# Other places for tiles, slices and loads in the projections and scan of a hybrid encoder block

## The chip, the cores and the metric

The kernel runs on one core of a Trainium2 chip, as one program in one launch. The metric is the device time of one execution in microseconds (us). Before the change three executions took 2998.09, 3004.99 and 3011.6 us; their median, 3004.99 us, is the time to predict against. The profile is one further execution with its own time.

## The reference, cut to what matters

One encoder block over 1040 tokens (16 meta tokens, then 1024), width 1024. The part that the change touches is the input projection and the two-way state-space scan that is fed by it:

```python
u = rms_norm(h, w_norm_mix)
proj = einsum('btd,dk->btk', u, w_in)              # 72.5 column tiles of 128
c = depthwise_conv(conf_a * sigmoid(conf_g), 31)   # "conf": 8 tiles
xbc = silu(depthwise_conv(xbc, 7))                 # 16 tiles of x, 4 of B, 4 of C
gates = sigmoid(proj[gate])                        # 16 tiles
# z: 16 tiles, gates the scan's output; dt: 64 columns
# scan, per group g (4), chunk c (9), both directions:
cb = einsum('lgn,sgn->gls', C, B)                  # C times B, masked for each direction
y_diag = (cb * decay) @ (x * dt)
states = B.T @ (decay_to_end * x * dt);  y_off = C @ prev_state * exp(a_cs)
y = rms_norm((y_f + y_b + D * x) * silu(z))
```

Behind it come the output products of both branches, the merge, and a mixture of 16 experts with 128 MB of weights for each of its three matrices.

## The kernel before, in words

A Tile program: instructions are written in Python order, and the framework's scheduler places them on the engines by their priority (`tc.high_priority(offset=...)` moves an instruction ahead). What then stands on an engine runs strictly in that order.

**Front.** The 1040 tokens are handled in nine chunks (`TOK`: 16, then eight of 128). Per chunk: load `xt` (four buffers, loads on SP's and ACT's queues in turn), a Square with a sum on ACT (L265), square root and reciprocal, a scaling on DVE (L267), eight transposes on PE (L272), and the split into an upper and a lower f16 half, `uh` by ACT (L274) and `ul` by DVE (L275). `Columns` feeds the weights: a group of three column tiles of `w_in` is loaded at once, `scale` finds a power of two per tile (Squares on ACT L198, a product L204, small steps on DVE), `convert` makes the two f16 halves (ACT L225, DVE L226).

**Projections.** A column tile is made in three "thirds", one for each of three stretches of about 346 tokens. A third is 24 matmuls into one of three PSUM banks (`mm`): eight k-steps times three products of halves (L97 to L99). `do_dt` takes dt's 64 columns first and builds the decays. `first` is the list of tiles made before the scan, `plan[0]` to `plan[2]` carry the tiles of groups 1 to 3 beside the scan of groups 0 to 2, `plan[3]` what is left beside the scan of group 3.

- `x_(g, i)`, a channel tile (i of 0 to 3 are x, 4 is B, 5 is C): evacuated by ACT to `pre`, then six taps of the 7-wide convolution on DVE (L385, tile `po`), a Silu on ACT (L386). Eight thirds later PE transposes `po` (`turn`, L400, into a bank of `mm`), ACT copies the result (`xt`, L404), and it is written to `xk_d`, from which the next group's scan loads it.
- `c_(j)`, a conf tile: six thirds, then 30 taps of the 31-wide convolution on DVE (L339, tile `co`). They are kept in a list, and every step of the scan takes 2, 4, 3 or 6 of them, by group.
- `z_` and `g_` are evacuated by ACT (z with one product on DVE, L362).

**Scan.** 18 steps for each group. A step has `within` (the masked `cb`, L602 and L606; the decays `row`, L611 to L614; products `py`, L626) and `state` (`yo` L665, `st` L671, the state `S` on DVE). Between the two `fill` lets PE make as many thirds as the step's share of the group's plan. `cb` had a PSUM tile of its own in a pool with one buffer; its two masks are made by DVE.

Of the kernel before, what the change touches and what calls it, by code (L numbers as in the profile page):

```python
# [7 lines left out]
F32 = mybir.dt.float32  # L8
# [4 lines left out]
AF = mybir.ActivationFunctionType  # L13
# [19 lines left out]
NTT = len(TOK)  # L33
# [12 lines left out]
def tile_block(ctx, tc, x, meta_tokens, w_norm_mix, w_in, w_conf_dw, b_conf_dw, conf_ln_g, conf_ln_b,  # L46
# [100 lines left out]
    def power(dst, src, up, down):  # L147

        dve.tensor_scalar(dst[:, down], src, 32.0, 2.0 ** -110, op0=OP.mult, op1=OP.max)
        di = dst.bitcast(I32)  # L150
        dve.tensor_scalar(di[:, down], di[:, down], 23, 23, op0=OP.logical_shift_right, op1=OP.logical_shift_left)
        dve.tensor_scalar(di[:, up], di[:, down], -1.0, float(268 << 23), op0=OP.mult, op1=OP.add)
        dve.tensor_scalar(di[:, down], di[:, down], float(14 << 23), None, op0=OP.subtract)
# [10 lines left out]
    with tpool("upool", side="right") as upool, tpool("stage", bufs=4, side="right") as stage, \  # L164
# [11 lines left out]
        class Columns:  # L176
# [52 lines left out]
            def take(self, col):  # L229

                n = self.at
                assert self.order[n] == col
                self.at += 1
                if n == 0:
                    self.load()
                    self.scale(0, turned)
                    self.convert(0)
                if n % self.G == 0:
                    self.load()
                if n % self.G == 1:  # L240
                    self.scale(n - 1 + self.G)
                self.convert(n + 1)
                wh, wl, sc = self.split.pop(n)
                return wh, wl, sc[:, 2:3], sc[:, 3:4]

        columns = Columns()
        wtile = columns.take


        with tpool("a_sb", bufs=2) as sb, tpool("a_ps", bufs=4, space=PSUM) as aps:  # L250
            wmix = sb.tile([P, D], F32, name="wmix", bufs=1)
            nc.scalar.dma_start(wmix, w_norm_mix[0].partition_broadcast(P))
            wabs = sb.tile([P, D], F32, name="scr")
            act.activation(out=wabs, in_=wmix, func=AF.Abs)
            wmax = sb.tile([P, 1], F32, name="wmax", bufs=1)
            dve.tensor_reduce(out=wmax, in_=wabs, axis=AX.X, op=OP.max)

            power(su, wmax, slice(0, 1), slice(1, 2))
            for c, (t0, L) in enumerate(TOK):
                xt = sb.tile([P, D], F32, name="xt", bufs=4)  # L260
                eng = nc.scalar if c % 2 else nc.sync
                eng.dma_start(xt[:L], meta_tokens if c == 0 else x[0, t0 - 16:t0 - 16 + L])
                scr = sb.tile([P, D], F32, name="scr")
                ss = sb.tile([P, 1], F32, name="ss")
                act.activation(out=scr[:L], in_=xt[:L], func=AF.Square, accum_out=ss[:L])  # L265
                rsqrt_mean(ss[:L], ss[:L], D)
                dve.scalar_tensor_tensor(xt[:L], xt[:L], ss[:L], wmix[:L], op0=OP.mult, op1=OP.mult)  # L267
                for q in range(2):
                    ps = aps.tile([P, 4, P], F32, name="tp")
                    for j in range(4):  # L270
                        k = 4 * q + j
                        turned = pe.transpose(ps[:, j, :L], xt[:L, k * P:(k + 1) * P], ident[:L, :L])  # L272
                    uu = uh[:, 4 * q:4 * q + 4, t0:t0 + L]
                    act.activation(out=uu, in_=ps[:, :, :L], func=AF.Copy, scale=su[:, 0:1])  # L274
                    dve.scalar_tensor_tensor(ul[:, 4 * q:4 * q + 4, t0:t0 + L], ps[:, :, :L], su[:, 0:1], uu,  # L275
                                             op0=OP.mult, op1=OP.subtract)
            prow = sb.tile([36, D], F32, name="prow", bufs=1)
            nc.gpsimd.dma_start(prow[:TK], w_conf_dw[0])
            nc.gpsimd.dma_start(prow[31:32], b_conf_dw)
            nc.gpsimd.dma_start(prow[32:33], conf_ln_g)  # L280
            nc.gpsimd.dma_start(prow[33:34], conf_ln_b)
            nc.gpsimd.dma_start(prow[34:36], w_ssm_norm[0].rearrange("(r c) -> r c", r=2))
            srow = sb.tile([8, 3 * D], F32, name="srow", bufs=1)
            nc.gpsimd.dma_start(srow[:TS], w_ssm_conv[0])
            nc.gpsimd.dma_start(srow[7:8], b_ssm_conv)
            db = sb.tile([P, H], F32, name="db", bufs=1)
            nc.gpsimd.dma_start(db, ssm_d[0].partition_broadcast(P))
            for hh in range(2):
                dve.tensor_copy(d2[64 * hh:64 * hh + 64], db[64 * hh:64 * hh + 64, hh::2])
            ps = aps.tile([P, KD, 36], F32, name="tp")  # L290
            for j in range(KD):
                pe.transpose(ps[:, j], prow[:, j * P:(j + 1) * P], ident[:36, :36])
            dve.tensor_copy(cp, ps)
            dve.tensor_scalar_mul(cp[:, :, 0:TK], cp[:, :, 0:TK], 0.5)
            ps = aps.tile([P, 24, 8], F32, name="tp")
            for j in range(24):
                pe.transpose(ps[:, j], srow[:, j * P:(j + 1) * P], ident[:8, :8])
            dve.tensor_copy(sp, ps)

        def proj(wsplit, t0, n):  # L300
            ps = mps.tile([P, 512], F32, name="mm")
            wh, wl = wsplit[:2]
            mm3(ps[:, :n], lambda k: wh[:, k, :], lambda k: wl[:, k, :],
                lambda k: uh[:, k, t0:t0 + n], lambda k: ul[:, k, t0:t0 + n], KD)
            return ps[:, :n]

        def soon():
            return tc.high_priority(offset=1000)
# [102 lines left out]


        def do_dt(b1, b1ps):
            w = wtile(OFF_DT)
            v, ve = [b1.tile([64, T], F32, name=n_, bufs=1) for n_ in ("dtv", "dte")]
            for t0, n in NCH0:
                act.activation(out=v[:, t0:t0 + n], in_=proj(w, t0, n)[:64], func=AF.Copy,
                               scale=w[2][:64])
            dtb = b1.tile([P, 2, 64], F32, name="dtb", bufs=1)
            for i, a in enumerate((ssm_dt_bias, ssm_a_log)):  # L420
                nc.gpsimd.dma_start(dtb[:, i], a[0].rearrange("d h -> (d h)").partition_broadcast(P))
# [61 lines left out]
                nc.gpsimd.dma_start(ecs_d[1:, hh].rearrange("c q l -> q c l"),  # L483
                                    ve[hh::2, NMETA:].rearrange("h (c l) -> h c l", l=P))


        def x_(g, *tiles):
            return [("xbc", g, i) for i in tiles]

        def z_(*js):  # L490
            return [("z", j) for j in js]

        def g_(*js):
            return [("gate", j) for j in js]

        def c_(j):
            return [("conf", j)]

        first = x_(0, 4) + c_(0) + x_(0, 5, 0) + g_(0) + x_(0, 1, 2) + g_(1) + x_(0, 3) + z_(0, 1, 2)
        plan = [x_(1, 4) + z_(3) + x_(1, 5, 0) + c_(1) + x_(1, 1) + g_(2) + x_(1, 2, 3) + g_(3, 4) + z_(4, 5),  # L500
                x_(2, 4) + z_(6) + c_(2) + z_(7) + x_(2, 5, 0, 1) + g_(5) + x_(2, 2, 3) + c_(3) + z_(8, 9),
                x_(3, 4) + z_(10) + x_(3, 5) + z_(11) + c_(4) + x_(3, 0, 1) + g_(6) + x_(3, 2, 3) + g_(7, 8) + z_(12, 13),
                z_(14, 15) + c_(5) + g_(9) + c_(6) + g_(10, 11) + c_(7) + g_(12, 13, 14, 15)]
        makers = {"conf": do_conf, "xbc": xbc_tile, "z": z_tile, "gate": gate_tile}
        columns.order.append(OFF_DT)
        for kind, *a in first + [i for p_ in plan for i in p_]:
            if kind == "conf":
                columns.order += [a[0] * P, D + a[0] * P]
            elif kind == "xbc":
                columns.order.append(OFF_XBC + (4 * a[0] + a[1], 16 + a[0], 20 + a[0])[max(0, a[1] - 3)] * P)  # L510
            else:
                columns.order.append((OFF_Z if kind == "z" else OFF_GATE) + a[0] * P)

        def thirds(items):
            for kind, *a in items:
                for _ in makers[kind](*a):
# [5 lines left out]
        with tpool("b1") as b1:  # L522
# [12 lines left out]
            with tpool("s2", bufs=2) as s2, tpool("sps", bufs=1, space=PSUM) as sps:  # L535
# [45 lines left out]
                    nc.gpsimd.dma_start(yz_d[g][:, :, t0:t0 + L].rearrange("i p t -> p i t"), xa)  # L581

                shared = {}

                def within(g, c, d):

# [820 lines left out]
```

## Time and profile before

| | us |
|---|---|
| median of three executions | 3004.99 |
| the profiled execution | 2988.87 |
| its span in the profile | 2987.1 |
| PE busy, of the span | 2750.6 (92%) |
| DVE busy | 2240.1 (75%) |
| ACT busy | 1713.3 (57%) |

PE is TensorE, DVE is VectorE, ACT is ScalarE, POOL is GpSimd, SP is SyncE. Matmuls are pipelined, so two rows may overlap; a wait stands in brackets at the end of a row of a timeline, with what ended it. The granted clock is TensorE's, as a share of its full speed.

### The profile page before, as it was taken

The numbers are of one execution on the slowest core, as the hardware profiler recorded it, in microseconds if no ns is written. First come the engines' busy times: TensorE is split into PE (matmuls) and PEld (weight loads), VectorE is DVE, ScalarE is ACT, GpSimd is POOL, SyncE is SP. The second block draws the span as 40 slices with busy tenths as digits, with TensorE's granted clock in tenths as the row PEclk, the third lists the DMA queues.
The fourth block names the chain that finished last, engine by engine and source line by source line (L and its number), as shares of the span: only waits on it lengthen the run. The fifth ranks groups of instructions, "written<-read, shape, count | busy, mean of one in ns | idle before, by whom it ended". The sixth has DMA issues, their size and how long they took to land. (4 is left out here: it accounts for less than half of the span.)

```text
span 2987.1 us, 65478 instructions
## 1 busy us (share of the span) xinstructions
PE 2750.6 (92%) x27584; PEld 2359.5 (79%) x27584; DVE 2240.1 (75%) x3023; ACT 1713.3 (57%) x2549; POOL 616.6 (21%) x688
## 2 busy tenths in 40 slices
PE   6989989989997998989998889999999999999995
PEld 4656656655665666989967889999999999999995
DVE  6867896998896799988456677777767676777663
ACT  6567656565665542444223656766666666666743
POOL 2131132132123113330000002222211112222213
PEclk8999989999998999999999899999999999999997
DMA  5356576565566554424345889999999999999994
GB/s 146 96 160 198 173 214 202 156 197 181 181 180 207 161 176 131 161 61 139 107 141 181 301 291 332 337 327 333 336 322 330 325 332 322 332 338 330 334 323 141
DMA packets 337783, 689.77 MB, mean 231 GB/s; under 512 B 38241, under 2 KB 98049, under 8 KB 337481
## 3 DMA queue, kind: packets, MB, share of 16 engines
q1 hardware_dynamic: 284784, 528.74, 51.4%
q0 software_dynamic: 42624, 125.45, 14.7%
q10 hardware_dynamic: 10080, 31.40, 3.3%
q8 instruction: 216, 3.54, 0.5%
q14 instruction: 79, 0.65, 0.1%
HBM read 610.48 MB, written 75.01 MB: 229 GB/s over the span
## 5 line engine op out<-in xcount | busy, mean ns | idle before, releaser
L97 PE MATMUL gu<-xT,wh 128*128 128x130 f16 x3968 | 698.1, 222 | 2.3 <-ACT sil L1180 2.3
L98 PE MATMUL gu<-xT,wh 128*128 128x130 f16 x3968 | 697.9, 220 | 0.0
L99 PE MATMUL gu<-xT,wl 128*128 128x130 f16 x3968 | 697.1, 220 | 0.8 <-DVE wl L1151 0.8
L1137 ACT ACTIVATE junk<-wst 128x2048 bf16<-128x2048 f32 x248 | 473.7, 1910 | 386.3 <-DMA wst<-in_w_exp_gate_dram 313.1
L1151 DVE SCALAR_TENSOR_TENSOR wl<-wst,sc,wh 128x2048 f16<-128x2048 f32 x248 | 572.7, 2346 | 24.3 <-ACT wh L1148 20.7
L98 PEld LDWEIGHTS <-wh 128*128 128x128 f16 x4856 | 480.4, 99 | 75.5 <-issue 32.6
L97 PEld LDWEIGHTS <-wh 128*128 128x128 f16 x4856 | 474.7, 98 | 52.1 <-issue 9.7
L99 PEld LDWEIGHTS <-wl 128*128 128x128 f16 x4832 | 470.0, 97 | 45.2 <-DVE wl L1151 1.1
L1203 PE MATMUL dn<-ac,wst 128*128 128x130 f32 x3840 | 459.3, 277 | 0.0
L1203 PEld LDWEIGHTS dn<-ac,wst 128*128 128x128 f32 x3840 | 440.7, 191 | 0.0
L1222 POOL DMA_INDIRECT h<-yo,idx x60 | 181.5, 3025 | 910.2 <-DVE yo L1221 758.5
L339 DVE SCALAR_TENSOR_TENSOR co<-ci,ct,co 128x1040 f32<-128x1040 f32 x240 | 323.8, 1349 | 5.5 <-ACT co L336 3.8
L97 PE MATMUL mm<-uh,wh 128*128 128x346 f16 (+3 forms) x888 | 279.4, 315 | 17.4 <-ACT xt L404 8.1
L97 PE MATMUL mm<-uh,wl 128*128 128x346 f16 (+1 forms) x864 | 271.7, 314 | 13.3 <-ACT xt L404 7.0
L98 PE MATMUL mm<-ul,wh 128*128 128x346 f16 (+3 forms) x888 | 279.0, 314 | 0.0
L99 PE MATMUL mm<-uh,wh 128*128 128x346 f16 (+3 forms) x888 | 278.1, 314 | 0.0
L98 PE MATMUL mm<-ul,wl 128*128 128x346 f16 (+1 forms) x864 | 271.2, 314 | 0.0
L99 PE MATMUL mm<-uh,wl 128*128 128x346 f16 (+1 forms) x864 | 271.0, 314 | 0.0
L611 ACT ACTIVATE row<-row,cst 128x128 f32<-128x128 f32 (+1 forms) x576 | 170.8, 378 | 143.4 <-DMA row<-cs_d 123.9
L1148 ACT ACTIVATE wh<-wst,sc 128x2048 f16<-128x2048 f32 x124 | 241.2, 1994 | 16.1 <-DVE sc L1114 15.4
L385 DVE SCALAR_TENSOR_TENSOR po<-pre,sp,po 128x1040 f32<-128x1040 f32 x144 | 185.7, 1296 | 2.4 <-ACT po L382 2.0
L97 PE MATMUL mm<-yh,wh 128*128 128x346 f32 (+1 forms) x480 | 156.9, 333 | 15.6 <-ACT yh L796 8.4
(431 smaller groups left out, 4839.9 us busy)
## 6 DMA issues: line engine op xcount, KB each, us to landing
wst<-in_w_exp_gate_dram SPq DMA_DIRECT2D x128, 1024.0 KB, 7.9
wst<-in_w_exp_up_dram SPq DMA_DIRECT2D x128, 1024.0 KB, 9.7
wst<-in_w_exp_down_dram SPq DMA_DIRECT2D x128, 1024.0 KB, 9.9
wr<-in_w_in_dram POOLq DMA_DIRECT2D x70, 512.0 KB, 6.4
row<-cs_d SPq DMA_DIRECT2D x64, 512.0 KB, 5.0
xk<-xk_d SPq DMA_DIRECT2D x92, 256.0 KB, 3.5
er<-ecs_d SPq DMA_DIRECT2D x120, 128.0 KB, 3.7
xk_d<-xt POOLq DMA_DIRECT2D x40, 256.0 KB, 4.2
```

What stands on the lines that cost most here:

```text
L97: pe.matmul(ps, wh(k), xh(k), start=(k == 0), stop=False)
L98: pe.matmul(ps, wh(k), xl(k), start=False, stop=False)
L99: pe.matmul(ps, wl(k), xh(k), start=False, stop=(k == K - 1))
L339: dve.scalar_tensor_tensor(co, ci[:, m:m + T], ct[:, m:m + 1], co, op0=OP.mult, op1=OP.add)
L385: dve.scalar_tensor_tensor(po, pre[:, m:m + T], sp[:, j, m:m + 1], po, op0=OP.mult, op1=OP.add)
L611: act.activation(out=E[:L, j, :L], in_=E[:L, j, :L], func=AF.Relu, scale=-1.0, bias=cs)
L1137: act.activation(out=junk, in_=t[m][b], func=AF.Square, accum_out=sq[:, b, m:m + 1])
L1148: act.activation(out=wh[m][0], in_=t[m][0], func=AF.Copy, scale=sc[:, 1, m:m + 1])
L1151: dve.scalar_tensor_tensor(wl[m][b], t[m][b], sc[:, 1, m:m + 1], wh[m][b], op0=OP.mult, op1=OP.subtract)
L1203: pe.matmul(last["dn"][b // 3][:, b % 3], t[:, k, b * P:b * P + P], ac[:, 2 * i + k], start=(i + k == 0 and b % 3 == 0), stop=(i == 7 and ...
L1222: nc.gpsimd.indirect_dma_start(out=h2_d[b], in_=yo[:, h], in_offset=None, compute_op=OP.add, out_offset=bass.IndirectOffsetOnAxis(ap=r.idx ...
```

## The change

Four things are done.

1. **The plan.** In `plan[0]` to `plan[2]` the conf tile that stood among the channel tiles goes behind them or nearer to their end, so the last channel tile of a group now stands at third 27 of 42 (was 30), 30 of 45 (was 33) and 27 of 45 (was 33). In `plan[3]` one conf tile changes place with a gate tile, so the last conf tile stands three thirds earlier.
2. **C times B.** One PSUM tile of four 128-wide slices (one bank) is kept for the whole scan, and `cb` takes the slices in turn, instead of a one-buffer tile for each chunk.
3. **x.** All nine chunks have a buffer, so that all loads are issued at the start. The first weights' loads are issued behind them.
4. **dt.** The scaling and conversion of the first weights, and dt's three products, are written between the chunks, each product as soon as its tokens (chunks 0 to 2, 3 to 5, 6 to 8) are transposed; `do_dt` only evacuates them.

```diff
-        plan = [x_(1, 4) + z_(3) + x_(1, 5, 0) + c_(1) + x_(1, 1) + g_(2) + x_(1, 2, 3) + g_(3, 4) + z_(4, 5),
+        plan = [x_(1, 4) + z_(3) + x_(1, 5, 0) + g_(2) + x_(1, 1, 2) + g_(3) + x_(1, 3) + c_(1) + z_(4, 5) + g_(4),
...
-                if n == 0:
-                    self.load()
-                    self.scale(0, turned)
-                    self.convert(0)
...
+            xts = []
             for c, (t0, L) in enumerate(TOK):
-                xt = sb.tile([P, D], F32, name="xt", bufs=4)
+                xts.append(sb.tile([P, D], F32, name="xt", bufs=NTT))
                 eng = nc.scalar if c % 2 else nc.sync
...
+            columns.load()
...
+                if c == 2:
+                    columns.scale(0, turned)
+                    columns.convert(0)
+                    w_dt = wtile(OFF_DT)
+                if c in (2, 5, 8):
+                    dts.append(proj(w_dt, *NCH0[c // 3]))
...
-            for t0, n in NCH0:
-                act.activation(out=v[:, t0:t0 + n], in_=proj(w, t0, n)[:64], func=AF.Copy,
-                               scale=w[2][:64])
+            for (t0, n), ps in zip(NCH0, dts):
+                act.activation(out=v[:, t0:t0 + n], in_=ps[:64], func=AF.Copy, scale=w_dt[2][:64])
...
+                cb, cbs = sps.tile([P, 4, P], F32, name="cb"), [0]
...
-                        ps = sps.tile([P, P], F32, name="cb")
+                        ps = cb[:, cbs[0] % 4]
+                        cbs[0] += 1
```

On PE, before, where `plan[0]` ends and group 0's scan goes over to group 1's (`mm<-ident,po` is a turn of a channel tile, the rows of L97 on are a third):

```order
L671 MATMUL st<-xw,Bk 128x512
L665 MATMUL yo<-Cc,S_4199 128x128 x4
L602 MATMUL cb<-bc__4392 16x16
L400 MATMUL mm<-ident,po 16x128
L400 MATMUL mm<-ident,po 128x128 x8
L665 MATMUL yo<-Cc,S_4349 128x16 x4
L602 MATMUL cb<-bc__4650 128x128
L626 MATMUL py<-row,xw 64x128 x16
L400 MATMUL mm<-ident,po 16x128
L400 MATMUL mm<-ident,po 128x128 x8
L602 MATMUL cb<-bc__4924 128x128
L97 LDWEIGHTS wl
```

The same place in the changed program:

```order
L436 MATMUL mm<-ident,po 16x128
L436 MATMUL mm<-ident,po 128x128 x4
L611 MATMUL cb<-bc__4104 128x128
L635 MATMUL py<-row,xw 64x128 x8
L674 MATMUL yo<-Cc,S_4073 128x128 x4
L680 MATMUL st<-xw,Bk 128x512
L674 MATMUL yo<-Cc,S_4202 128x128
L436 MATMUL mm<-ident,po 128x128 x4
L97 LDWEIGHTS wl
L97 MATMUL mm<-uh,wl 128x346
```

Before, two channel tiles' turns and three `cb` stand with no third between them; now one tile's turns stand there, and thirds follow at once.

On DVE, before, where the last two channel tiles of group 1 are convolved (`po<-pre`) and a conf tile's taps (`co<-ci`) stand among them:

```order
L385 SCALAR_TENSOR_TENSOR po<-pre,sp,po 128x1040
L339 SCALAR_TENSOR_TENSOR co<-ci,ct,co 128x1040
L385 SCALAR_TENSOR_TENSOR po<-pre,sp,po 128x1040
L568 TENSOR_TENSOR xa<-xa,py 128x512
L667 TENSOR_TENSOR er<-yo,er 128x512
L385 SCALAR_TENSOR_TENSOR po<-pre,sp,po 128x1040
L679 TENSOR_TENSOR S_4073<-st,S_4073 128x512
L550 TENSOR_TENSOR xw<-xk,dtw 128x512
L339 SCALAR_TENSOR_TENSOR co<-ci,ct,co 128x1040
L385 SCALAR_TENSOR_TENSOR po<-pre,sp,po 128x1040
```

In the changed program, the last channel tile of group 1:

```order
L421 SCALAR_TENSOR_TENSOR po<-pre,sp,po 128x1040 x3
L366 SCALAR_TENSOR_TENSOR ci<-sg,mm 128x348
L676 TENSOR_TENSOR er<-yo,er 128x512
L421 SCALAR_TENSOR_TENSOR po<-pre,sp,po 128x1040
L688 TENSOR_TENSOR S_3920<-st,S_3920 128x512
L557 TENSOR_TENSOR xw<-xk,dtw 128x512
L575 TENSOR_TENSOR xa<-xa,er 128x512
L421 SCALAR_TENSOR_TENSOR po<-pre,sp,po 128x1040
L201 CAST sqb<-sq 128x3
L686 TENSOR_TENSOR S_4202<-S_3920,etot 128x512
L615 TENSOR_TENSOR cbm_3970<-cb,tri_le 128x128
```

Before, the taps of `co` alternate with the convolution; now none stands ahead of the last convolution there. Counted over the whole order, ahead of the last convolution of group 1, 2 and 3 stand 51, 90 and 144 taps of `co` before, and 30, 75 and 120 now; ahead of the same convolution's first turn stand 77, 122 and 167 thirds before, and 77, 122 and 164 now.

On PE, before, at the front (`tp<-ident,xt` are the transposes of x, `prow` and `srow` those of small parameters, `mm<-sqb` the product of `scale`, and with `mm<-uh` dt's products begin):

```order
L272 MATMUL tp<-ident,xt 128x16 x8
L272 MATMUL tp<-ident,xt 128x128 x64
L204 LDWEIGHTS onesb
L204 MATMUL mm<-sqb,onesb 128x3
L292 MATMUL tp<-ident,prow 128x36 x8
L297 MATMUL tp<-ident,srow 128x8 x24
L97 LDWEIGHTS wh
L97 MATMUL mm<-uh,wh 128x272
```

In the changed program:

```order
L308 MATMUL tp<-ident,xt 128x16 x8
L308 MATMUL tp<-ident,xt 128x128 x48
L204 LDWEIGHTS onesb
L204 MATMUL mm<-sqb,onesb 128x3
L308 MATMUL tp<-ident,xt 128x128 x8
L97 LDWEIGHTS wh
L97 MATMUL mm<-uh,wh 128x272
L98 LDWEIGHTS wh
L98 MATMUL mm<-ul,wh 128x272
```

Two of dt's three products now stand ahead of the last chunk's eight transposes which, with those of the parameters, follow behind these two. On ACT, the conversion of the first three weight tiles (L225) moves ahead of the last two chunks' evacuations, and the Squares of the third group of weights move ahead of the last chunk's. On POOL's queue the loads of the second group of weights go ahead of the small parameters' loads, and those of the third group ahead of dt's bias; on SP's queue two of the first three weight loads go behind the x loads.

## Rows read from the trace of the kernel before

**Rows 1.** Busy time of the engines over the whole span, from the page
```profile
PE 2750.6 (92%) x27584; PEld 2359.5 (79%) x27584; DVE 2240.1 (75%) x3023; ACT 1713.3 (57%) x2549; POOL 616.6 (21%) x688
```

**Rows 2.** Busy time by stretch: stretch, length, busy time by engine, granted clock, DMA share, GB/s
```profile
45.00:1177.00 1132.00, 1034.42 (x7356) 697.74 (x7355) 943.16 (x1291) 669.89 (x1310) 261.28 (x432) 0.96 0.58 173
...
1690.00:2987.00 1297.00, 1227.01 (x17230) 1216.76 (x17227) 903.09 (x1079) 819.74 (x908) 266.87 (x102) 0.98 0.91 318
```

**Rows 3.** First load of an expert's weights, from the queue's timeline
```profile
1620.88 0.94 SPq L1127 DMA_DIRECT2D wst<-in_w_exp_gate_dram  x2
```

**Rows 4.** PE's waits, from its timeline: start, length, instruction, [wait before it and releaser]
```profile
414.14 2.09 PE L400 MATMUL mm<-ident,po 128*16 128x128 f32 x9 [4.50 <-ACT po L386]
...
579.59 2.08 PE L671 MATMUL st<-xw,Bk 128*128 128x512 f32 x2 [3.65 <-DVE S L679]
...
630.34 0.28 PE L400 MATMUL mm<-ident,po 128*16 128x128 f32 x1 [4.61 <-ACT po L386]
...
676.87 2.09 PE L400 MATMUL mm<-ident,po 128*16 128x128 f32 x9 [6.66 <-ACT po L386]
...
909.69 2.09 PE L400 MATMUL mm<-ident,po 128*16 128x128 f32 x9 [6.69 <-ACT po L386]
...
930.47 2.09 PE L400 MATMUL mm<-ident,po 128*16 128x128 f32 x9 [10.40 <-ACT po L386]
...
935.08 0.45 PE L97 MATMUL mm<-uh,wl 128*128 128x346 f16 x1 [2.10 <-ACT xt L404]
```

**Rows 5.** Busy time by stretch, the three clumps of waits
```profile
409.00:436.00 27.00, 17.93 (x102) 13.30 (x102) 22.43 (x39) 19.87 (x41) 10.09 (x17) 0.68 0.78 236
664.00:692.00 28.00, 16.58 (x101) 11.53 (x98) 12.99 (x23) 22.02 (x39) 14.95 (x25) 0.70 0.79 238
900.00:940.00 40.00, 18.88 (x110) 14.97 (x109) 29.85 (x46) 24.99 (x47) 12.81 (x19) 0.66 0.64 187
```

**Rows 6.** Busy time by stretch, where VectorE is full and where it has room
```profile
350.00:425.00 75.00, 66.02 (x483) 47.11 (x480) 75.00 (x103) 46.75 (x94) 20.82 (x33) 0.93 0.64 184
525.00:625.00 100.00, 89.95 (x653) 61.92 (x652) 99.80 (x132) 59.87 (x119) 14.18 (x24) 0.97 0.59 173
...
925.00:1025.00 100.00, 90.87 (x642) 60.20 (x643) 54.66 (x90) 58.78 (x120) 26.33 (x40) 0.93 0.64 196
1025.00:1150.00 125.00, 125.00 (x926) 85.14 (x925) 123.83 (x172) 52.44 (x112) 18.86 (x31) 1.00 0.50 152
```

**Rows 7.** VectorE's groups by line: busy us, mean ns, idle before them
```profile
L339 DVE SCALAR_TENSOR_TENSOR co<-ci,ct,co 128x1040 f32<-128x1040 f32 x240 | 323.8, 1349 | 5.5 <-ACT co L336 3.8
L385 DVE SCALAR_TENSOR_TENSOR po<-pre,sp,po 128x1040 f32<-128x1040 f32 x144 | 185.7, 1296 | 2.4 <-ACT po L382 2.0
```

**Rows 8.** Two PE rows of one third, 23 products apart
```profile
386.00 0.31 PE L97 MATMUL mm<-uh,wh 128*128 128x346 f16 x1 [1.80 <-ACT xt L404]
...
389.37 0.31 PE L99 MATMUL mm<-uh,wh 128*128 128x346 f16 x1
```

**Rows 9.** PE's waits for VectorE's masks, from the list of waits: us, times, longest
```profile
PE cb L602 <- DVE cbm L606: 10.0, 7, 2.4
```

**Rows 10.** The front's timeline: conversion of the first weights, and their first product
```profile
43.52 1.15 ACT L225 ACTIVATE wh<-wr,sc 128x1024 f16<-128x1024 f32 x1 [1.33 <-DVE sc L211]
...
45.06 0.41 PE L97 MATMUL mm<-uh,wh 128*128 128x272 f16 x1
```

**Rows 11.** First and last start of a product with the weights in wl, by line 97
```profile
L97 PE MATMUL mm<-uh,wl x864: 307/310/495, 59.1 to 1157.8; 128*128 128x346 f16 x115, 128*128 128x348 f16 x58
```

**Rows 12.** The front's timeline on ScalarE: an x load awaited, a sqrt, an evacuation, a Square
```profile
23.67 1.06 ACT L265 ACTIVATE scr<-xt 128x1024 f32<-128x1024 f32 x1 [0.89 <-DMA xt<-in_x_dram]
...
25.29 0.28 ACT L102 ACTIVATE ss<-ss,eps 128x1 f32<-128x1 f32 x1
...
25.48 0.67 ACT L274 ACTIVATE uh<-tp,su 128x512 f16<-128x512 f32 x1
...
26.23 1.05 ACT L198 ACTIVATE junk<-wr 128x1024 bf16<-128x1024 f32 x1
```

More of the change, by code (lines that the diff above doesn't have):

```diff
@@ L247, in tile_block, with proj, x_, z_ @@
         wtile = columns.take
+        def proj(wsplit, t0, n):
+            ps = mps.tile([P, 512], F32, name="mm")
+            wh, wl = wsplit[:2]
+            mm3(ps[:, :n], lambda k: wh[:, k, :], lambda k: wl[:, k, :],
+                lambda k: uh[:, k, t0:t0 + n], lambda k: ul[:, k, t0:t0 + n], KD)
+            return ps[:, :n]
+        def x_(g, *tiles):
+            return [("xbc", g, i) for i in tiles]
+        def z_(*js):
+            return [("z", j) for j in js]
+        def g_(*js):
+            return [("gate", j) for j in js]
+        def c_(j):
+            return [("conf", j)]
+        first = x_(0, 4) + c_(0) + x_(0, 5, 0) + g_(0) + x_(0, 1, 2) + g_(1) + x_(0, 3) + z_(0, 1, 2)
+        plan = [x_(1, 4) + z_(3) + x_(1, 5, 0) + g_(2) + x_(1, 1, 2) + g_(3) + x_(1, 3) + c_(1) + z_(4, 5) + g_(4),
+                x_(2, 4) + z_(6) + x_(2, 5) + z_(7) + x_(2, 0, 1) + c_(2) + x_(2, 2, 3) + g_(5) + c_(3) + z_(8, 9),
+                x_(3, 4) + z_(10) + x_(3, 5) + z_(11) + x_(3, 0, 1) + g_(6) + x_(3, 2, 3) + c_(4) + z_(12, 13) + g_(7, 8),
+                z_(14, 15) + c_(5) + g_(9) + c_(6) + g_(10) + c_(7) + g_(11, 12, 13, 14, 15)]
+        columns.order.append(OFF_DT)
+        for kind, *a in first + [i for p_ in plan for i in p_]:
+            if kind == "conf":
+                columns.order += [a[0] * P, D + a[0] * P]
+            elif kind == "xbc":
+                columns.order.append(OFF_XBC + (4 * a[0] + a[1], 16 + a[0], 20 + a[0])[max(0, a[1] - 3)] * P)
+            else:
+                columns.order.append((OFF_Z if kind == "z" else OFF_GATE) + a[0] * P)
+        dts = []
         with tpool("a_sb", bufs=2) as sb, tpool("a_ps", bufs=4, space=PSUM) as aps:
@@ L258, in tile_block @@
             power(su, wmax, slice(0, 1), slice(1, 2))
+            xts = []
             for c, (t0, L) in enumerate(TOK):
-                xt = sb.tile([P, D], F32, name="xt", bufs=4)
+                xts.append(sb.tile([P, D], F32, name="xt", bufs=NTT))
                 eng = nc.scalar if c % 2 else nc.sync
-                eng.dma_start(xt[:L], meta_tokens if c == 0 else x[0, t0 - 16:t0 - 16 + L])
+                eng.dma_start(xts[c][:L], meta_tokens if c == 0 else x[0, t0 - 16:t0 - 16 + L])
+            columns.load()
+            for c, (t0, L) in enumerate(TOK):
+                xt = xts[c]
                 scr = sb.tile([P, D], F32, name="scr")
@@ L298, in tile_block @@
             dve.tensor_copy(sp, ps)
[L300 to L305, printed above, removed]
         def soon():
@@ L413, in do_dt @@
         def do_dt(b1, b1ps):
-            w = wtile(OFF_DT)
             v, ve = [b1.tile([64, T], F32, name=n_, bufs=1) for n_ in ("dtv", "dte")]
-            for t0, n in NCH0:
-                act.activation(out=v[:, t0:t0 + n], in_=proj(w, t0, n)[:64], func=AF.Copy,
-                               scale=w[2][:64])
+            for (t0, n), ps in zip(NCH0, dts):
+                act.activation(out=v[:, t0:t0 + n], in_=ps[:64], func=AF.Copy, scale=w_dt[2][:64])
             dtb = b1.tile([P, 2, 64], F32, name="dtb", bufs=1)
@@ L484, in do_dt @@
                                     ve[hh::2, NMETA:].rearrange("h (c l) -> h c l", l=P))
[L487 to L499, printed above, removed]
-        plan = [x_(1, 4) + z_(3) + x_(1, 5, 0) + c_(1) + x_(1, 1) + g_(2) + x_(1, 2, 3) + g_(3, 4) + z_(4, 5),
-                x_(2, 4) + z_(6) + c_(2) + z_(7) + x_(2, 5, 0, 1) + g_(5) + x_(2, 2, 3) + c_(3) + z_(8, 9),
-                x_(3, 4) + z_(10) + x_(3, 5) + z_(11) + c_(4) + x_(3, 0, 1) + g_(6) + x_(3, 2, 3) + g_(7, 8) + z_(12, 13),
-                z_(14, 15) + c_(5) + g_(9) + c_(6) + g_(10, 11) + c_(7) + g_(12, 13, 14, 15)]
-        makers = {"conf": do_conf, "xbc": xbc_tile, "z": z_tile, "gate": gate_tile}
[L505 to L512, printed above, removed]
+        makers = {"conf": do_conf, "xbc": xbc_tile, "z": z_tile, "gate": gate_tile}
         def thirds(items):
```

## The prediction

> **What bounds the kernel now.** I read the busy times first, then PE's waits in order of time, then busy time and granted clock by stretch around each wait, then what DVE does there. Over the span PE is busy 92%, DVE 75% [rows 1]. The change lies in the first 1177 us. From 45 to 1177 us PE is busy 1034 of 1132 us at a mean granted clock of 0.96, so about 98 us are waits and some 40 us (4% of 1034) go to stretches at half clock [rows 2]. What follows is a chain of its own: the experts' stage is busy on PE in 1227 of 1297 us with the DMA engines 91% busy [rows 2], and its first weights are fetched at 1621 us, long after the scan [rows 3]. So I take a shift of the scan's end to reach the end one for one.
>
> Where are the 98 us? The longest waits of the projections and scan stand where one group's scan goes over to the next: 4.50 us at 414, 6.66 at 677, and 6.69, 10.40 and 2.10 around 910 to 935; nearly all are a turn of a channel tile that waits for the Silu (ACT po L386) behind its convolution [rows 4]. The stretches around the three places make this a sum: PE idles 27.0 - 17.93 = 9.1 us, 28.0 - 16.58 = 11.4 us and 40.0 - 18.88 = 21.1 us, together 41.6 us. Its granted clock is 0.68, 0.70 and 0.66 there; so of its busy time about 17.93 x 0.32 + 16.58 x 0.30 + 18.88 x 0.34 = 17.1 us are lost to the level of 1.2 instead of 2.4 GHz (the granted clock is a mean over the stretch, so this is rough) [rows 5]. I call these places the three clumps. ACT is the releaser by name only: what is late is DVE. It is busy 75.0 of 75 us before the first clump and 99.8 of 100 ahead of the second; behind the third it has 100 - 54.7 = 45.3 us of room, and from 1025 to 1150 none [rows 6].
>
> **The plan.** What occupies DVE there is in part work that nothing waits for: 30 taps of 1.349 us for each conf tile, beside 6 of 1.296 us for each channel tile [rows 7]. In the order of before the taps alternate with the convolutions of the last channel tiles. The change puts the conf tile behind them, and so ahead of the last convolution of group 1, 2 and 3 stand 21, 15 and 24 taps fewer (51 to 30, 90 to 75, 144 to 120). These are counts from the start, so they don't add up: the taps that leave the first clump come back later.
>
> - First clump: 21 x 1.349 = 28.3 us less on DVE, against a wait of 9.1 us. It should go, and the thirds that now stand beside the turns keep PE at work.
> - At the third clump, which closes the account: 24 x 1.349 = 32.4 us less on DVE ahead of the last convolution. If DVE still sets the time of that place, PE gets there 32.4 us earlier. But it has made 164 thirds instead of 167 by then. A third is 24 products, 23 of which take 3.37 us [rows 8], so 3.5 us; 3 x 3.5 = 10.6 us of PE are still to be done. Gain: 32.4 - 10.6 = 21.8 us. The waits of the second clump are in this sum.
> - Low clock: what is lost behind the third clump (18.88 x 0.34 = 6.4 us) falls behind that place, so it is not yet in the sum. I take half of it, 3.2 us, since the waits shrink and don't vanish.
> - The 24 taps must be made in the last group: 32.4 us into a room of 45.3 us. I take them as hidden, by PE's products from 925 to 1025. If that cover is gone they cost up to 32.4 us.
> - Bounds: from 32.4 us slower (taps late, nothing gained) to all three clumps gone with their low clock and the two lone waits at 580 and 630: 41.6 + 17.1 + 3.65 + 4.61 = 67 us. I take 25 (21.8 + 3.2), near the middle, because it is the value that DVE's own rows give.
>
> **C times B in four slices.** PE waited 10.0 us in all, seven times, for DVE to read the masks' source before it wrote the next `cb` [rows 9]; most of it inside the clumps. In the changed program each `cb` still waits until both masks of the `cb` before are made, so four slices let nothing start earlier, and the edit alone moves nothing on PE. Zero; bounds 0 and the 10.0. The Trainium skill (PSUM — Partial Sum Buffer, "PSUM bank collisions raise a hardware error") says that two engines may not touch one bank in the same 32 partitions at once, whatever their columns, so that a slice beside one that DVE reads is no freer than the slice itself. By that rule the term is 0 as well, and without it up to 10.0; no row here shows a collision, since every `cb` waits.
>
> **x at once, and dt among the transposes.** Before, the first weights are converted at 43.52 us and dt's products start at 45.06 [rows 10], when all transposes are done; the next tile's product follows at its earliest with wl at 59.1 [rows 11], so dt takes 14.0 us, part of it at half clock. ACT sets the pace of the front: its row of the one x load that it awaits shows only 0.89 us [rows 12]. Ahead of the conversion ACT now has one sqrt (0.28), four evacuations (4 x 0.67) and one Square of weights (1.05) less: 4.0 us; with the x wait some 5 us. So the first product starts near 40. Two of the three products (656 of 1040 columns, 14.0 x 0.63 = 8.8 us) end near 49; the last chunk's transposes, evacuations and split then take about 3 us with the parameters' transposes among them, and the third product (384 columns, 24 x 0.16 = 3.8 us at full clock) with half of the next tile's third (1.8) ends near 57.5, where before that point is 59.1 + 1.8. Gain 3.4; I take 2, because on ACT the last chunk's evacuation now stands behind three Squares of weights whose loads are issued on POOL's queue only when the first conversions free their buffers, and this queue's other loads (dt's bias) wait behind them. Two of SP's first weight loads go behind x; they are wanted by the scaling only after the seventh chunk. Bounds: 6 gained, 3 lost.
>
> **The sum.** 25 + 0 + 2 = 27 us. The profiled execution took 2988.87 us, 16.1 below the median of the runs, 3004.99. 2988.9 - 27 = 2962; against the median 3005 - 27 = **2978 us**.
>
> **The rivals.**
>
> A, everything at the clumps goes. DVE is not the bound once its work is even, and PE runs through. For it: with thirds beside the turns PE always has something else. Against: DVE is at 99 to 100% over long stretches, so it has little to spare. 41.6 + 17.1 + 2 = 61 us: 2944.
>
> B, DVE starves first. Taps that come later leave it idle where they stood (groups 0 and 2, first half), and it reaches the third clump hardly sooner. If 19 of the 32.4 us are idled away, 21.8 - 19 = 3 remain, with 3.2 of clock and 2 at the front: 8 us, 2997. For it: PE and DVE wait for each other in turns, and DVE did have room outside the full stretches. Against: the room stood behind the clumps, where PE had been stalled.
>
> C, slower: the waits scatter. Each turn now stands alone between thirds and waits for its own convolution; the 41.6 us remain as a sum but fall in some nine places (three late tiles in each of three groups) in place of three, and each has its own stretch at 1.2 GHz. At 17.1 / 3 = 5.7 us per place that is 9 x 5.7 - 17.1 = 34 us more, less 2 at the front: 3037. It decides against the change as soon as the waits stay whole and stand in more than three places. For it: the lone 4.61 us at 630 shows that one turn alone can wait. Against: 24 taps less ahead of them.
>
> That the change doesn't do what it says holds for the slices; it is in the sum.
>
> **Chances.** Forecast 0.55 (own range 2962 to 2993), A 0.17, B 0.20, C 0.08. A measurement of this kernel can tell 0.5%, 15 us, from no change. Faster by more than that: the forecast but for a little of its upper end, and A, and none of B: 0.71. Within: B and that end, 0.21. Slower: C, 0.08. The range takes in A and B and leaves C and what is beyond A out: 2940 to 3004.
>
> **What would show it.** In the profile of the changed kernel, PE's waits before turns near 410, 660 and 900 us: under 10 us for the three together if the step on the plan is right, with a granted clock above 0.85 around them. DVE's room behind the third clump shrinks from 45 us to 15 to 25. The `cb` waits fall with the clumps, not by the slices. dt's first product starts before 42 us. The prediction is wrong if the scan ends less than 10 us earlier or DVE's taps hold up the first output products, and if waits before turns stand in many places with the clock low after each, C was right.

## The result and the profile after

The changed kernel took 2973.87 us (four runs, 2969.78 to 2977.84) against 3001.59 us (four runs, 2998.09 to 3011.6) for the kernel before: a ratio of 0.9904, 95% interval 0.9888 to 0.9921. On a second chip a copy of it took 2967.93 us (six runs) against 2989.8 us (17 runs), 0.9927 [0.9906, 0.9947]. It is faster, by 22 to 28 us of medians.

The profiled executions differ by less: 2988.87 us before and 2973.07 after, 15.8 us. The one of before lay 12.7 us below its median, the one of after 0.8 us. So the traces can account for about 16 us; the rest of the 28 is the spread of the kernel before.

The projections and scan of the changed kernel, the counterpart of the first stretch of [rows 2] (columns as there):

```profile
45.00:1163.00 1118.00, 1032.82 (x7357) 694.44 (x7356) 944.49 (x1295) 670.13 (x1313) 257.68 (x427) 0.96 0.59 175
```

DVE's work up to the next stage is the same (943 us before, 944 now), and PE's nearly so; the stage is 14 us shorter because both idle less. In the queue's timeline of the changed kernel the experts' first weights are fetched 16.6 us earlier than in [rows 3], so the shift does go through to the end:

```profile
1604.28 0.94 SPq L1136 DMA_DIRECT2D wst<-in_w_exp_gate_dram  x2
```

The places of the three clumps, as stretches of the changed kernel (counterparts of [rows 5]), and then DVE's full and empty stretches (counterparts of [rows 6]):

```profile
400.00:430.00 30.00, 29.92 (x228) 20.82 (x227) 26.50 (x41) 16.88 (x40) 13.06 (x20) 1.00 0.83 223
645.00:680.00 35.00, 30.53 (x212) 21.42 (x208) 27.26 (x39) 21.23 (x44) 16.03 (x24) 0.90 0.88 255
895.00:930.00 35.00, 28.79 (x205) 19.48 (x204) 31.20 (x51) 23.51 (x43) 18.30 (x27) 0.95 0.94 268
```
```profile
350.00:425.00 75.00, 69.92 (x495) 47.30 (x495) 59.09 (x91) 48.78 (x101) 25.50 (x39) 0.95 0.73 209
525.00:625.00 100.00, 91.41 (x657) 63.06 (x655) 88.28 (x122) 66.31 (x128) 17.10 (x27) 0.97 0.61 180
925.00:1025.00 100.00, 99.97 (x726) 66.07 (x725) 85.57 (x119) 54.38 (x117) 20.34 (x33) 1.00 0.64 186
1025.00:1150.00 125.00, 124.41 (x931) 85.30 (x929) 124.72 (x165) 44.60 (x96) 22.94 (x37) 1.00 0.50 150
```

PE idles 0.1, 4.5 and 6.2 us in the three, 10.8 together where it was 41.6, and the granted clock is 1.00, 0.90 and 0.95 where it was near 0.68. (The third stretch begins behind a wait of 4.78 us that belongs to its clump; see the account of the prediction.) Behind the third, PE now runs full from 925 to 1150, on DVE's 14.4 us of room instead of 45. But that is not yet the gain. PE's waits by releaser up to the last projection (us in all, times, longest), first of before, then of the changed kernel, show where they went:

```profile
PE mm L400 <- ACT po L386: 35.4, 7, 10.4
PE mm L97 <- ACT xt L404: 15.0, 10, 4.6
PE cb L602 <- DVE cbm L606: 10.0, 7, 2.4
PE mm L97 <- ACT pre L379: 8.4, 5, 2.9
PE mm L400 <- ACT pre L379: 6.3, 5, 3.1
```
```profile
PE mm L436 <- ACT pre L415: 16.8, 5, 6.2
PE mm L97 <- ACT pre L415: 16.1, 8, 5.0
PE mm L436 <- ACT po L422: 14.2, 4, 4.8
PE mm L97 <- ACT xt L440: 8.4, 4, 4.6
PE cb L611 <- DVE cbm L615: 3.2, 4, 1.2
```

The turns' wait for Silu fell by 21.2 us, those on `xt` and `cb` by 6.6 and 6.8; the waits for `pre`, ScalarE's evacuation of a projection, rose from 14.7 to 32.9 (30.2 and 31.5 in the profiles of after_again and plan_only below). That is 16.4 net. The new waits in PE's timeline of the changed kernel:

```profile
365.79 0.45 PE L97 MATMUL mm<-uh,wh 128*128 128x346 f16 x1 [4.99 <-ACT pre L415]
...
588.19 1.12 PE L436 MATMUL mm<-ident,po 128*128 128x128 f32 x4 [6.23 <-ACT pre L415]
...
734.56 0.45 PE L97 MATMUL mm<-uh,wh 128*128 128x346 f16 x1 [3.60 <-ACT pre L415]
...
841.75 1.11 PE L436 MATMUL mm<-ident,po 128*128 128x128 f32 x4 [6.14 <-ACT pre L415]
```

Follow the last one back, first on ACT and then on SP's queue, both in the changed kernel:

```profile
833.64 2.45 ACT L620 ACTIVATE row<-row,cst 128x128 f32<-128x128 f32 x8 [3.74 <-DMA row<-cs_d]
836.44 2.44 ACT L620 ACTIVATE row<-row,cst 128x128 f32<-128x128 f32 x8 [0.36 <-DMA row<-cs_d]
838.90 1.28 ACT L621 ACT_TABLE_LOAD   x1
840.20 1.06 ACT L621 ACTIVATE row<-row 128x1024 f32<-128x1024 f32 x1
841.16 0.97 ACT L415 ACTIVATE pre<-mm,sc 128x348 f32<-128x348 f32 x2
```
```profile
811.84 0.33 SPq L550 DMA_DIRECT2D xk<-xk_d  x1
826.41 0.33 SPq L649 DMA_DIRECT2D Bk<-xk_d  x1
...
828.60 1.19 SPq L599 DMA_DIRECT2D row<-cs_d  x2
```

SP stands for 14 us at one load (`Bk`, whose buffer a state product `st` on PE frees), the two decay rows behind it are issued at 828.6, ACT waits for them because they come before `pre` in its list, and does both rows and an Exp before the evacuation that PE needs. Ahead of the other three waits, too, ACT stood at a decay row whose load came late:

```profile
354.98 2.45 ACT L620 ACTIVATE row<-row,cst 128x128 f32<-128x128 f32 x8 [4.20 <-DMA row<-cs_d]
...
585.25 2.45 ACT L620 ACTIVATE row<-row,cst 128x128 f32<-128x128 f32 x8 [3.31 <-DMA row<-cs_d]
...
731.62 2.45 ACT L620 ACTIVATE row<-row,cst 128x128 f32<-128x128 f32 x8 [9.44 <-DMA row<-cs_d]
```

ACT's waits for such rows are 160.4 us in all now, 123.9 before (142.6 in after_again, so the size of the rise is not sure).

### The profile page after: what moved, and what is told of

Its sections match the earlier page's. It is cut to its first block, busy times and chain, and to the rows that moved or that the text cites. A ratio compares the mean times of both kernels' runs of the same rounds, so it can differ in the third digit from the quotient of the medians.

```text
span 2971.3 us, 65492 instructions
## 1 busy us (share of the span) xinstructions
PE 2752.8 (93%) x27584; PEld 2358.3 (79%) x27584; DVE 2244.9 (76%) x3023; ACT 1711.6 (58%) x2551; POOL 621.8 (21%) x688
## 5 line engine op out<-in xcount | busy, mean ns | idle before, releaser
L97 PE MATMUL gu<-xT,wh 128*128 128x130 f16 x3968 | 701.1, 223 | 3.2 <-ACT sil L1189 3.2
L1160 DVE SCALAR_TENSOR_TENSOR wl<-wst,sc,wh 128x2048 f16<-128x2048 f32 x248 | 572.4, 2346 | 21.8 <-ACT wh L1157 18.6
L97 PEld LDWEIGHTS <-wh 128*128 128x128 f16 x4856 | 476.6, 98 | 55.8 <-issue 12.0
L97 PE MATMUL mm<-uh,wh 128*128 128x346 f16 (+3 forms) x888 | 282.8, 318 | 26.7 <-ACT pre L415 13.0
L99 PE MATMUL mm<-uh,wh 128*128 128x346 f16 (+3 forms) x888 | 281.4, 317 | 0.0
L97 PE MATMUL mm<-uh,wl 128*128 128x346 f16 (+1 forms) x864 | 271.3, 314 | 6.2 <-ACT pre L415 3.1
L620 ACT ACTIVATE row<-row,cst 128x128 f32<-128x128 f32 (+1 forms) x576 | 170.6, 377 | 176.8 <-DMA row<-cs_d 160.4
L1157 ACT ACTIVATE wh<-wst,sc 128x2048 f16<-128x2048 f32 x124 | 241.4, 1996 | 22.1 <-DVE sc L1123 21.4
L97 PE MATMUL mm<-yh,wh 128*128 128x346 f32 (+1 forms) x480 | 158.0, 335 | 17.3 <-ACT yh L805 12.5
```

The source lines that it names most:

```text
L620: act.activation(out=E[:L, j, :L], in_=E[:L, j, :L], func=AF.Relu, scale=-1.0, bias=cs)
L1157: act.activation(out=wh[m][0], in_=t[m][0], func=AF.Copy, scale=sc[:, 1, m:m + 1])
L1160: dve.scalar_tensor_tensor(wl[m][b], t[m][b], sc[:, 1, m:m + 1], wh[m][b], op0=OP.mult, op1=OP.subtract)
```

## The experiments

Ten kernels were run. The table gives, for one profiled execution each, when the last product of certain thirds starts, minus the kernel before (us; a third is 24 projection products, counted along PE's timeline, dt's among them). Thirds 79, 123 and 171 are the ones just behind the clumps, 211 is near the last. cb_only, nowhere here more than 2.8 us from the kernel before, is left out.

| third | before, at | after | after_again | plan_only | front_only | plan_g1 | plan_g3 | half_taps | bk4 | taps_later | c3_late |
|---|---|---|---|---|---|---|---|---|---|---|---|
| 79 | 437.5 | -12.9 | -14.3 | -15.0 | -0.2 | -16.2 | -4.5 | -23.0 | -16.9 | -13.0 | -10.2 |
| 123 | 687.1 | -25.9 | -27.5 | -27.4 | +13.1 | -3.4 | -1.3 | -32.1 | -31.2 | -34.1 | -30.0 |
| 171 | 950.5 | -17.2 | -19.1 | -20.3 | +16.6 | -5.5 | -25.2 | -46.9 | -25.4 | -34.5 | -42.9 |
| 211 | 1135.4 | -18.3 | -20.3 | -17.0 | +19.7 | -2.4 | -15.7 | -32.6 | -26.0 | -16.0 | -2.1 |

The theory: VectorE's list is one backlog, so what counts is how many taps stand ahead of the last convolution before the third clump. The rivals: each clump is a price of its own; or not VectorE but ScalarE's order and the loads set the pace.

**after_again**: the whole change, unedited.

> The whole change once more, beside the kernel before on one chip. Theory 1 (the gain is in the projections and scan): ratio 0.990 plus or minus 0.002 and PE's last third some 18 us earlier than before, as in its first trace. Rival (part of the first ratio is the spread of the kernel before, whose profiled execution was 12.7 us under its median): ratio near 0.994, the 16 us that the two traces differ by.

0.9927 [0.9906, 0.9947], given above: between the two expectations, with an interval that takes in both. The last thirds come 20.3 us earlier, as the first says; the kernel before is faster here (median 2989.8) than in the first comparison, as the second says.

**plan_only, front_only, cb_only**: one part of the change each.

```diff
 plan_only: before, with the four rows of `plan` of the change
 front_only: before, with
-                xt = sb.tile([P, D], F32, name="xt", bufs=4)
+                xts.append(sb.tile([P, D], F32, name="xt", bufs=NTT))
+                if c in (2, 5, 8):
+                    dts.append(proj(w_dt, *NCH0[c // 3]))
 cb_only: before, with
-                        ps = sps.tile([P, P], F32, name="cb")
+                        ps = cb[:, cbs[0] % 4]
```

> Only the new places of the conf and gate tiles; the front and the cb tile as before. Theory 1 (the plan is all of the gain): within 0.2% of the whole change's ratio, the first two clumps of waits gone, and new waits of PE for ACT's evacuation near 365, 588, 735 and 840 us. Rival (the front's lead carries on): 3 to 6 us slower than the whole change.

> Only x at once and dt's products among the transposes. Theory 1: the front's lead of about 3 us at the first third with wl is gone by the start of the scan, because the decays' chain and not PE sets it; ratio 1.000 plus or minus 0.001. Rival: the lead stays, ratio 0.998 to 0.999.

> Only the four slices for C times B. Theory 1: the order on PE and the waits are as before, ratio 1.000 plus or minus 0.0015, 10 us of waits of cb for cbm as before. Rival (slices free PE earlier): these waits fall below 4 us and the time by 4 to 10 us.

The plan alone gives 0.9926 [0.9904, 0.9948], all of the gain within the interval, with the new waits for `pre` at 364, 585, 735 and 837 us. The slices alone give 1.0007 [0.9987, 1.0027], and PE's waits for the masks stay at 10.3 us (10.0 before). The Trainium skill (PSUM — Partial Sum Buffer, "PSUM bank collisions raise a hardware error") says that a different address in the same bank and the same 32 partitions still collides; by that, slices of one bank are no freer than one. cb_only's waits agree, but no run here parts the rule from the program's own waits, since no `cb` in that trace starts before both masks of the one before have ended.

The front alone is slower: 1.0063 [1.0039, 1.0086], which no theory expected. At third 3 it is exactly where before is (0.0); it is 2.0 us early at third 103 and 13.1 late at third 123, 500 us behind the lines that were edited, and stays late. One of PE's two long waits there (the other is 10.77 us at 646.67), and ACT's timeline ahead of it, in the front_only kernel:

```profile
614.71 0.38 PE L436 MATMUL mm<-ident,po 128*16 128x128 f32 x1 [9.80 <-ACT po L422]
```
```profile
608.73 2.45 ACT L618 ACTIVATE row<-row,cst 128x128 f32<-128x128 f32 x8 [6.19 <-DMA row<-cs_d]
611.21 1.06 ACT L619 ACTIVATE row<-row 128x1024 f32<-128x1024 f32 x1
612.29 1.28 ACT L422 ACT_TABLE_LOAD   x1
613.58 1.07 ACT L422 ACTIVATE po<-po 128x1040 f32<-128x1040 f32 x1
```

No line of the scan was edited, yet the framework's scheduler put its instructions in another order; here ACT waits 6.19 us for a decay row and only then makes the `po` that PE wants. With the new plan the list comes out otherwise, and the front moves nothing (plan_only against the whole change). Which line of the front tips the order was not taken apart.

**plan_g1, plan_g3**: the first row of the new plan alone, and the last two alone.

```diff
 plan_g1: before, with
-        plan = [x_(1, 4) + z_(3) + x_(1, 5, 0) + c_(1) + x_(1, 1) + g_(2) + x_(1, 2, 3) + g_(3, 4) + z_(4, 5),
+        plan = [x_(1, 4) + z_(3) + x_(1, 5, 0) + g_(2) + x_(1, 1, 2) + g_(3) + x_(1, 3) + c_(1) + z_(4, 5) + g_(4),
 plan_g3: before, with
-                x_(3, 4) + z_(10) + x_(3, 5) + z_(11) + c_(4) + x_(3, 0, 1) + g_(6) + x_(3, 2, 3) + g_(7, 8) + z_(12, 13),
+                x_(3, 4) + z_(10) + x_(3, 5) + z_(11) + x_(3, 0, 1) + g_(6) + x_(3, 2, 3) + c_(4) + z_(12, 13) + g_(7, 8),
 and the last row
```

> The kernel before with the first row of the plan alone taken from the change (conf 1 and two gate tiles later in group 1). Theory (VectorE's list is one backlog: taps held back from one clump must be done ahead of the next, since VectorE has no room between them): the projections' third 79 comes 12 to 15 us earlier, as in the whole change, and nearly all of that is given back by third 123 to 127 (0 to 5 us early there); the time is 0.998 to 1.001 of the kernel before. Rival (each clump's wait is a price of its own): the 12 to 15 us stay to the end and the time is 0.995 to 0.996.

> The kernel before with the last two rows of the plan alone taken from the change (conf 4 behind the channel tiles of group 3's turns, and the tail). Theory (one backlog on VectorE that is settled at the third clump, where fewer taps stand ahead of the last convolution): thirds up to 151 run as before (within 3 us), the last projection product comes 12 to 20 us earlier, and the time is 0.993 to 0.996, most of what the whole plan gives (0.9926). Rival (the gain is made at the first two clumps, and the third only keeps it): the time is 0.999 to 1.002.

This settles the first rival. plan_g1 takes 16.2 us out of the first clump, more than the whole change does, and has 3.4 left at third 123: 1.0011 [0.9988, 1.0034], nothing. plan_g3 runs within 5 us of before up to the second clump, is 25.2 us early behind the third, keeps 15.7 of that at third 211 and ends at 0.9945 [0.9927, 0.9963]. A clump's wait that is taken away ahead of another clump is only lent.

**half_taps**: the changed kernel with 15 taps instead of 30.

```diff
-            taps.extend([lambda m=m: tap(m) for m in range(1, TK)])
+            taps.extend([lambda m=m: tap(m) for m in range(1, TK, 2)])
```

> The changed kernel with every other tap of the depthwise convolution left out (15 taps a tile instead of 30; its result is not the reference's): 120 taps at 1.35 us, 162 us, fewer on VectorE. Theory (VectorE's backlog still sets the changed kernel's scan): the last projection product comes 25 to 60 us earlier than in the changed kernel, and the waits on ACT pre and ACT po shrink with it; the time is 0.980 to 0.992 of the change's 2967.9 us, 0.973 to 0.985 of the kernel before. Rival (ACT's order and the row loads, or TensorE's own work, now set it): at most 10 us earlier, and the time is 0.989 to 0.993 of the kernel before.

2951.11 us, 0.9871 [0.9838, 0.9904], 17 us below the changed kernel by medians taken beside equal ones of before (2989.66 and 2989.8): between the two expectations, in the time as in the thirds. Ahead of third 171 stand 60 taps fewer, some 80 us of VectorE, and it comes 29.7 us earlier than in the changed kernel; 14.3 are left at third 211. PE's waits for `pre` up to the last projection fall little (27.5 us where the change has 32.9), those for `po` more (5.9 where it has 14.2), and DVE now waits itself. Three rows of that list, of the half_taps kernel:

```profile
DVE po L421 <- ACT po L418: 24.9, 12, 6.6
PE mm L97 <- ACT pre L415: 17.1, 10, 4.4
...
PE mm L436 <- ACT pre L415: 10.4, 4, 6.0
```

So VectorE still sets part of the changed kernel's time, and most of the waits for `pre` are not due to VectorE's taps.

**bk4**: one more buffer for the load at which SP stood.

```diff
-                        Bk = s2.tile([P, P], F32, name="Bk", bufs=3)
+                        Bk = s2.tile([P, P], F32, name="Bk", bufs=4)
```

> The changed kernel with four buffers for the scan's B rows (Bk) instead of three; only SP's order of loads differs. Theory (SP's queue stands at Bk's load, which waits for a state product, the rows behind it come late, ACT waits for them in order, and TensorE waits for ACT): SP's waits Bk <- PE st fall from 65 to under 25 us, ACT's row <- DMA row from 160 to 125 to 145 us, the 6.1 us wait near 841 us is gone, and the time falls by 3 to 9 us against the changed kernel (0.990 of the kernel before against 0.9927). Rival (the queue stops as long at its next load, xk <- xw, er <- xa or row <- py, whose buffers VectorE and TensorE free): SP's total of waits stays within 20 us and the time within 2 us of the changed kernel's (0.992 to 0.9935).

0.9929 [0.9902, 0.9956]: the same time, as the rival has it (its profiled execution, 2960.62, is the lowest of its six). Two of SP's waits, first of the changed kernel, then of bk4:

```profile
SPq L550 <- DVE xw L557: 184.2, 59, 9.8
...
SPq L649 <- PE st L680: 65.3, 31, 14.5
```
```profile
SPq L550 <- DVE xw L557: 193.0, 54, 9.9
...
SPq L649 <- PE st L680: 59.9, 30, 14.1
```

The suspected wait did not go away: with a fourth buffer the loads of `Bk` moved one place forward in SP's list and wait there for the same product. The 6.14 us at 841 are 5.74 here. The experiment therefore neither proves nor refutes the chain from SP over ACT to PE; it stands as read from the trace.

**taps_later, c3_late**: still more taps behind the third clump (114 and 90 ahead of it, where the change has 120).

```diff
 taps_later: after, with
-  c_(2) + x_(2, 2, 3) + g_(5) + c_(3) + z_(8, 9)  ...  x_(3, 2, 3) + c_(4) + z_(12, 13) + g_(7, 8)
+  x_(2, 2, 3) + g_(5) + c_(2) + z_(8, 9) + c_(3)  ...  x_(3, 2, 3) + g_(7, 8) + c_(4) + z_(12, 13)
-                    some_taps((2, 4, 3, 6)[g])
+                    some_taps((2, 3, 3, 7)[g])
 c3_late: after, with
-  g_(5) + c_(3) + z_(8, 9)  ...  c_(4) + z_(12, 13) + g_(7, 8)  ...  z_(14, 15) + c_(5)
+  g_(5, 6, 7) + z_(8, 9)  ...  c_(3) + z_(12, 13) + g_(9, 10)  ...  c_(4) + z_(14, 15) + c_(5)
```

> The changed kernel with conf 2, 3 and 4 each a few items later in the plan (and slower tap rates): 60 taps instead of 75 stand ahead of the last convolution of group 2, 114 instead of 120 ahead of that of group 3. Theory (one backlog on VectorE, settled at the third clump, with 14 us of VectorE room behind it): 6 taps at 1.35 us, 4 to 8 us earlier at third 171 and kept to the end; the time is 0.990 to 0.9915 of the kernel before (the change has 0.9927). Rival (ACT's order and the row loads hold the third clump now): 0.992 to 0.9945.

> The changed kernel with conf 3 moved behind group 3's channel tiles, conf 4 into the last row and gate tiles in their places: 90 taps instead of 120 ahead of the last convolution of group 3, so 40 us of VectorE work are moved behind the third clump, where 14 us of 100 are free. Theory (the backlog is moved, not removed): third 171 comes 10 to 30 us earlier than in the changed kernel, VectorE is full from there on and the next stage starts 0 to 15 us later than it would have kept; the time is 0.990 to 0.996 of the kernel before, no better than the change. Rival (after the third clump nothing waits for the taps, so all that the clump gives back stays): the next stage starts 10 us or more earlier than in the changed kernel and the time is 0.987 to 0.9895.

taps_later: 0.9921 [0.9893, 0.9949], c3_late: 0.9945 [0.9922, 0.9968]. Neither beats the change by more than its interval; of the kernels with all their taps none does. Both reach third 171 far ahead (17.3 and 25.7 us before the changed kernel; 4 to 8 and 10 to 30 were expected) and give it back between 1060 and 1130 us, taps_later against its expectation. First PE in c3_late and DVE ahead of it, then taps_later:

```profile
1123.55 0.45 PE L97 MATMUL mm<-uh,wh 128*128 128x346 f16 x1 [21.63 <-DVE ci L366]
```
```profile
1114.97 7.98 DVE L375 SCALAR_TENSOR_TENSOR co<-ci,ct,co 128x1040 f32<-128x1040 f32 x6
1122.99 0.94 DVE L366 SCALAR_TENSOR_TENSOR ci<-sg,mm 128x348 f32<-128x348 f32 x2
```
```profile
1050.00:1075.00 25.00, 21.55 (x152) 15.34 (x150) 24.96 (x37) 11.26 (x28) 1.73 (x3) 0.91 0.53 165
1075.00:1100.00 25.00, 16.44 (x114) 11.12 (x113) 25.00 (x38) 6.47 (x12) 5.53 (x10) 0.82 0.39 119
```

In c3_late DVE works off taps in a row while the next conf tile's `ci`, on which PE's buffers depend, stands behind them. In taps_later DVE is full, PE is not. The debt falls due at the end of the scan instead of at the clump.

## Why the prediction was right, and where its steps were off

- **The plan, 25 us (21.8 at the third clump, 3.2 of clock).** The mechanism holds: plan_only carries all of the gain, and plan_g1 shows that the first clump's 28 us of taps do come back, so that the third clump closes the account. By medians the plan is worth 22 us (2989.8 - 2967.45). But 21.8 came out with two parts that miss. VectorE up to the end of the last convolution of group 3, before and in the changed kernel (stretch, length, its busy time, granted clock, DMA share, GB/s):

```profile
0.00:919.05 919.05, 771.09 (x1061) 0.95 0.59 173
0.00:897.68 897.68, 737.83 (x1026) 0.95 0.60 175
```

  It is busy 33.3 us less, as said (32.4), but idles 159.8 us where it was 148.0, so the convolution ends 21.4 us earlier and not 32.4. That is rival B's step with 11.8 us in place of its 19; in plan_only, with 2.8 us more of idle time, the convolution ends 30.9 us earlier. In the changed kernel PE's lead at third 171 is 17.2 us, 4.2 less than the convolution's, where the three thirds still to be made were put at 10.6. In the four profiles with the whole plan as it is in the change that lead is 17.2, 19.1, 20.3 and 25.4 us, with 21.8 inside. (The 1.349 us of a tap is a mean that six taps of 3.3 to 3.5 us behind the scan pull up; the median is 1.296, and 24 taps are then 31.1 us.)
- **The low clock, 3.2.** Not borne out. From the program's start to the next stage's first product PE is busy 1053.42 us before, 1050.97 in the changed kernel, 1051.95 in after_again and 1053.62 in plan_only: 2.5 us less at most, and cb_only, which gains nothing, differs from before by 3.1. Around the clumps the clock did rise above 0.85 as said, but it fell elsewhere, from 800 to 850 us above all. There PE now waits 4.11, 3.30 and 6.14 us, at 808, 811 and 842 (before, then changed kernel, columns as in [rows 2]):

```profile
800.00:850.00 50.00, 49.42 (x360) 33.25 (x359) 47.85 (x60) 29.73 (x59) 6.41 (x9) 1.00 0.56 161
800.00:850.00 50.00, 34.59 (x216) 22.96 (x214) 43.71 (x61) 31.46 (x56) 8.98 (x16) 0.83 0.58 161
```

- **The three clumps' waits under 10 us.** Met only just. In the three stretches above, the waits of over 2.3 us are 4.47 and 2.35 us, but the turn that waited 6.69 us at 909.69 before [rows 4] now stands ahead of its stretch, and still waits:

```profile
876.54 0.39 PE L436 MATMUL mm<-ident,po 128*16 128x128 f32 x1 [4.78 <-ACT po L422]
```

  With it the turns' waits over 2.3 us are 9.25 us together. And rival C had a point that the forecast left out: from 350 us to the last projection nine waits of over 2.3 us, 40 us together, stand in the changed kernel, where before nine had 44. They did scatter, one stretch from 800 to 850 us at a lower clock with them. What C had wrong is the price, 34 us: what the new stretches cost, the clumps gave back, since PE's busy time did not grow.
- **The 24 taps hidden behind the third clump.** Right, with a little less room left than said (14.4, not 15 to 25). c3_late shows the price without that cover.
- **The slices, 0.** Right. The `cb` waits fell to 3.2 us with the clumps, and to 1.0 in plan_only, which has no slices.
- **The front, 2.** Wrong in size. dt's first product starts at 38.93 (said: before 42), the next tile's with `wl` at 56.2 instead of 59.1 [rows 11], but the two tiles' products now run mixed, and the last product of the third third starts when it did before (0.0). On the way PE waits 1.94 us for the last chunk's evacuation, the step on ACT that the text named, and then runs at a low clock where the text had counted dt's third product at the full one (the wait, and the same stretch before and in the changed kernel):

```profile
51.55 0.48 PE L97 MATMUL mm<-uh,wh 128*128 128x384 f16 x1 [1.94 <-ACT uh L310]
```
```profile
50.00:55.00 5.00, 5.00 (x33) 3.19 (x32) 0.00 (x0) 3.91 (x7) 0.00 (x0) 0.93 0.92 267
50.00:55.00 5.00, 3.15 (x10) 1.41 (x10) 2.18 (x6) 4.44 (x8) 0.00 (x0) 0.55 0.00 0
```

- **The shift of the scan's end reaching the end one for one.** Nearly: 18.3 us at the last projection, 14.7 at the next stage's first product (before it PE waits 9.95 us for ACT's `yh`, where before waits 6.41), 15.8 at the end.
- **Rival B** (VectorE starves first, 2997) is out as a total, though its step shows in part, as said. The total of the forecast is right, 2978 against 2973.87, because 25 for the plan is near the 22 of the medians and because the front's 2 is small. That it is this close is in part luck: 27 us were forecast and 27.7 measured by the first medians, but 21.9 on the second chip and 15.8 between the two profiled executions.

What the sum lacked is on ScalarE: once VectorE is nearer to being on time, PE waits for evacuations that stand in ACT's list behind loads that come late. That is the 18 us added to the waits for `pre`; half_taps shows that most of them stay when VectorE has time to spare. That the late loads are their cause is read from the traces and not shown by an experiment, since bk4 left these loads as late as they were; nor is it known what the time would be without these waits.

## What to carry to other kernels

Where an engine is full over several stages, count its work ahead of the last place where another engine waits for it; work moved out of an earlier wait is only lent, and comes due there. Before booking a relief as gain, read what stands ahead of the waited-for instruction on each engine that is next in line: an in-order list with a late load in it can be the next wait. And where a scheduler writes the lists, time each part of a change alone: here an edit at the start cost 20 us, lost half a millisecond later.

## What was not expected of the hardware

- The spread between executions of one kernel is as large as the effect: the kernel before ran between 2978.63 and 3000.49 us on the second chip, with the same program. One profile of each isn't enough to size 16 us; the thirds of several are.
- ACT's table loads took 1.28 us each, 22 of them ahead of the channel tiles' Silu (L422) and 20 ahead of the decay rows' Exp (L621). One of them is in the chain of a late evacuation (838.90).
